# Low halves of the weights: subtracted on GpSimd, or written as -hi by ScalarE and completed by an adding DMA

## The chip, the cores and the metric

The kernel runs on one core of a Trainium2 chip. The metric is the device time of one execution in microseconds. A difference of 0.3% is about 8.7 us.

## The reference, cut to what matters

A trunk of four layers over 528 positions (16 learned tokens in front of 512 frames) of width 1024, in float32. Each layer is a mixer and an MLP, each with a norm ahead of it and a residual after it:

```python
for layer in range(4):           # mixers: DeltaNet, attention, RG-LRU, DeltaNet
    u = rmsnorm(h, norm_mix_w[layer])
    h = h + mixer[layer % 3](u)  # w_in, the mixer's own work, w_out
    u = rmsnorm(h, norm_mlp_w[layer])
    h = h + square(relu(u @ w1[layer])) @ w2[layer]   # 1024 -> 4096 -> 1024
return rmsnorm(h, final_norm_w)
```

Most of the work is the products with weight matrices.

## The kernel before

**Products in three passes.** A float32 product is made from rounded operands (type float32r): the weight W is split into hi, its rounded value, and lo = W - hi, and the activation x the same way. `part` (line 372) issues three matmuls for each block of 128 rows: hi with x's high part, hi with x's low part, lo with x's high part. The 528 positions are done in two halves of 264 columns, so a full unit of weights (128 partitions x 1024, eight blocks of 128 columns) is 8 x 3 x 2 = 48 matmuls.

**Where weights come from.** The host lays all weights out in rows of `wts`, each 128 partitions x 2 units x 1024. `load` (line 293) fetches one row, 1 MB, from SP's queue into one of two buffers `raw`. `wsplit` (line 300) makes hi and lo of one unit: ScalarE copies raw to hi (line 309), and one engine, VectorE or GpSimd, subtracts (line 310). For a full unit hi and lo are two buffers of the pool `wp`, which has seven buffers in rotation; the first product of an MLP (`w1`) runs a scheme of seven products on half-size blocks, and its hi and lo share one buffer.

**Who subtracts.** `prep` (line 313) takes VectorE for the first two rows, and for `w2`, `lru_in`, `lru_out` and `lru_gate` VectorE for the first unit of a row and GpSimd for the second (LO_ENG, line 47). All other full units (`dn_ba`, `dn_in`, `dn_out`, `da_in`, `da_out`) are GpSimd's. That makes 82 units for VectorE and 188 for GpSimd. The 188 are 64 of `w2`, 62 of `dn_in` and `dn_ba`, 24 of `da_in`, 16 of `dn_out`, 8 of `da_out`, 8 of `lru_in`, 4 of `lru_out` and 2 of `lru_gate`. The half-size blocks of w1 are split by VectorE, one of seven by GpSimd; these stay.

**How far ahead.** `unit` (line 352) calls `prep` until six buffers' worth are waiting. With seven buffers in rotation, the lo of a full unit among full units takes the buffer that the unit three before it gives up.

**The MLP.** `mlp` (line 591) runs four groups: eight w1 units, then eight `w2` units that contract the group's eight hidden tiles. `open` (line 363) begins the first two units of `w2` on the first six tiles before the last two hidden tiles are ready.

**Order.** The program is written with background generators (`tick`, line 230) that advance the mixers' own work while products run. A scheduler then fixes the order of each engine's instructions ahead of the run; on the chip each engine works through its list in order and waits on semaphores. DMAs are issued from SP's queue (weights, and a few small transfers of DeltaNet through DRAM), and from GpSimd's (the transfers `gd`, `sa` and `vs` of the mixers).

Of the kernel before, what the change touches and what calls it, by code (L numbers as in the profile page):

```python
# [9 lines left out]
F32 = mybir.dt.float32  # L10
F32R = mybir.dt.float32r
AF = mybir.ActivationFunctionType
ALU = mybir.AluOpType
# [30 lines left out]
LATS = [1.7] * 8 + [1.1]  # L44
CORE_DMA = "gggsss"

LO_ENG = {"w2": "vg", "lru_in": "vg", "lru_out": "vg", "lru_gate": "vg"}

PRODS = (11, 21, 2, 3, 4, 1, 22)
OUT_PARTS = {"dn_out": (4, 4), "da_out": (4, 4), "lru_out": (8,)}  # L50
# [97 lines left out]
class K:  # L148
# [148 lines left out]
        m = len(self.rows[r])  # L297
        self.nc.sync.dma_start(raw[:, :m], self.wts[r, :, :m, :])

    def wsplit(self, src, lo_eng, names):  # L300

        nc = self.nc
        n = src.shape[1]
        if n == 512:
            t = self.wp.tile([128, 1024], F32R, tag="w", name=names)
            hi, lo = t[:, :512], t[:, 512:]
        else:
            hi, lo = (self.wp.tile([128, 1024], F32R, tag="w", name=f"{k}{names}") for k in ("hi", "lo"))
        nc.scalar.copy(hi, src)  # L309
        lo_eng.tensor_tensor(lo, src, hi.bitcast(F32), ALU.subtract)  # L310
        return hi, lo

    def prep(self):

        if self.wnext >= len(self.items):
            return
        nc = self.nc
        r, k = self.items[self.wnext]
        self.wnext += 1
        self.load(r)  # L320
        raw = self.raws[r]
        unit = self.rows[r][0]
        if unit[0] != "w1":
            key = self.rows[r][k]
            eng = nc.vector if r < 2 or LO_ENG.get(key[0], "gg")[k] == "v" else nc.gpsimd
            self.wq.append((key, 2) + self.wsplit(raw[:, k], eng, f"{r}_{k}"))
        else:
            A11, A12, A21, A22 = raw[:, 0, :512], raw[:, 0, 512:], raw[:, 1, :512], raw[:, 1, 512:]
            if k == 0:
                self.s12 = [self.L1(self.getl()), self.L1(self.getl())]  # L330
            S1, S2 = self.s12
            add = lambda o, a, b, op: self.sadd(k).tensor_tensor(o, a, b, op)  # L332
            if k == 2:
                add(S1, A21, A22, ALU.add)
                add(S2, S1, A11, ALU.subtract)
            elif k == 3:
                add(A21, A11, A21, ALU.subtract)
            elif k == 6:
                add(A12, A12, S2, ALU.subtract)
            src = (A11, A12, S2, A21, A22, S1, A12)[k]  # L340
            eng = nc.vector if k != 3 else nc.gpsimd
            self.wq.append((unit + (k,), 1) + self.wsplit(src, eng, f"op{r}_{k}"))
        if k == 0:
            self.load(r + 1)
# [1015 lines left out]
```

## Time and profile before

| | |
|---|---|
| median of 3 runs | 2884.54 us (2882.99 to 2892.52) |
| the profiled execution | 2883.85 us, span 2882.1 us |
| TensorE (PE) busy | 94% of the span, mean granted clock 0.965 |
| VectorE (DVE), ScalarE (ACT), GpSimd (POOL) busy | 72%, 45%, 32% |
| DMA | 241.11 MB, mean 84 GB/s |

PE is TensorE's matmuls, PEld its weight loads. A name with q (SPq, POOLq) is that engine's sequencer, which issues DMAs and waits. The stages by time: first DeltaNet layer to about 430 us and its MLP to 830, attention to 1120 and its MLP to 1500, RG-LRU to 1740 and its MLP to 2080, second DeltaNet to 2500 and the last MLP to the end.

### The profile page before, as it was taken

To read this page: it belongs to the slowest core of one execution; us is meant where nothing else is said; L and a number is where in the kernel's file an instruction comes from. 1 tells how busy PE (TensorE), PEld (TensorE's weight loads), DVE (VectorE), ACT (ScalarE), POOL (GpSimd) and SP (SyncE) were. 2 spreads that over 40 slices of the span, in tenths; PEclk is the share of its full clock that TensorE was granted. 3 is DMA by queue.
4 is the path that set the end of the run, shared out by engine and by line. 5 is a ranking of instruction groups with operands and counts; after the bars stand their busy time and mean duration, and the time that the engine had idled before them with its cause. 6 is when DMAs were issued, how large, how long until landed. Compare 5 with 4: busy or idle time off the path is not lost. (4 is left out here: it accounts for less than half of the span.)

```text
span 2882.1 us, 54564 instructions
## 1 busy us (share of the span) xinstructions
PE 2717.7 (94%) x22032; PEld 2627.1 (91%) x22032; DVE 2064.5 (72%) x4424; ACT 1291.2 (45%) x2856; POOL 918.0 (32%) x580
## 2 busy tenths in 40 slices
PE   7899998999999998999999889999998989999998
PEld 7898898999988887999998889999988888899997
DVE  6987749667735557876668987776589685677764
ACT  4454436334534444543354654443444554444433
POOL 4534333121243333211134532211454343422213
PEclk9999899999999999999999999999999899999999
DMA  4322212233331120322332112232223221132322
GB/s 145 90 79 73 58 50 76 90 102 103 103 105 64 56 66 31 103 89 88 103 103 74 68 65 97 95 103 89 89 89 93 64 67 52 52 103 95 110 89 74
DMA packets 74508, 241.11 MB, mean 84 GB/s; under 512 B 42278, under 2 KB 42824, under 8 KB 49040
## 3 DMA queue, kind: packets, MB, share of 16 engines
q1 hardware_dynamic: 68112, 222.46, 23.3%
q0 software_dynamic: 5488, 13.98, 2.0%
q8 instruction: 173, 2.83, 0.4%
q10 hardware_dynamic: 656, 1.18, 0.1%
q14 instruction: 79, 0.65, 0.1%
HBM read 229.23 MB, written 11.01 MB: 83 GB/s over the span
## 5 line engine op out<-in xcount | busy, mean ns | idle before, releaser
L310 POOL TENSOR_TENSOR lo<-raw,hi 128x1024 fp32r<-128x1024 f32 x188 | 460.0, 2447 | 836.2 <-PE d L219 450.1
L219 PE MATMUL c<-s,hi 128*128 128x264 f32 (+1 forms) x2768 | 511.7, 284 | 0.0
L219 PE MATMUL d<-s,hi 128*128 128x264 f32 (+1 forms) x2480 | 475.7, 289 | 36.1 <-DVE s L646 22.7
L309 ACT CAST hi<-raw 128x1024 fp32r<-128x1024 f32 x270 | 282.9, 1050 | 412.4 <-PE d L219 217.6
L219 PE MATMUL d<-uh,hi 128*128 128x264 f32 (+1 forms) x1520 | 453.9, 299 | 11.0 <-DVE s L646 10.9
L219 PE MATMUL d<-ul,hi 128*128 128x264 f32 (+1 forms) x1520 | 449.4, 296 | 0.0
L219 PE MATMUL d<-uh,lo 128*128 128x264 f32 (+1 forms) x1520 | 448.2, 295 | 0.0
L219 PEld LDWEIGHTS d<-s,hi 128*128 128x128 f32 x2480 | 391.9, 191 | 44.1 <-DVE s L646 19.0
L219 PEld LDWEIGHTS c<-s,hi 128*128 128x128 f32 x2768 | 430.1, 189 | 0.0
L219 PE MATMUL c<-s,lo 128*128 128x264 f32 (+1 forms) x1384 | 392.1, 284 | 0.0
L219 PE MATMUL d<-s,lo 128*128 128x264 f32 (+1 forms) x1240 | 357.4, 288 | 0.0
L219 PEld LDWEIGHTS d<-uh,hi 128*128 128x128 f32 x1520 | 298.2, 196 | 21.7 <-DVE s L646 14.1
L310 POOL TENSOR_TENSOR op<-raw,op 128x512 fp32r<-128x512 f32 x64 | 114.8, 1793 | 593.0 <-ACT op L309 582.0
L219 PEld LDWEIGHTS d<-uh,lo 128*128 128x128 f32 x1520 | 297.5, 196 | 5.0 <-issue 4.2
L219 PEld LDWEIGHTS d<-ul,hi 128*128 128x128 f32 x1520 | 297.8, 196 | 4.5 <-issue 3.5
L309 ACT CAST op<-raw 128x512 fp32r<-128x512 f32 x320 | 193.2, 619 | 237.2 <-PE c L219 119.4
L219 PEld LDWEIGHTS c<-s,lo 128*128 128x128 f32 x1384 | 261.1, 189 | 0.0
L219 PE MATMUL d<-s,op 128*128 128x264 f32 (+1 forms) x1788 | 242.2, 285 | 8.2 <-ACT s L485 3.8
L219 PEld LDWEIGHTS d<-s,lo 128*128 128x128 f32 x1240 | 237.4, 191 | 1.7 <-issue 1.5
L219 PEld LDWEIGHTS d<-s,op 128*128 128x128 f32 x1788 | 227.7, 190 | 9.7 <-ACT s L485 4.2
L310 DVE TENSOR_TENSOR op<-raw,op 128x512 fp32r<-128x512 f32 x256 | 222.4, 869 | 18.8 <-ACT op L309 18.7
L597 DVE TENSOR_TENSOR h<-h,c 128x264 f32<-128x264 f32 (+1 forms) x169 | 71.8, 425 | 184.2 <-PE c L219 184.0
(269 smaller groups left out, 5734.7 us busy)
## 6 DMA issues: line engine op xcount, KB each, us to landing
raw<-in_wts_dram SPq DMA_DIRECT2D x197, 1024.0 KB
s<-dimg SPq DMA_DIRECT2D x32, 245.0 KB
s<-gd POOLq DMA_DIRECT2D x16, 265.0 KB, 4.5
sa<-s POOLq DMA_DIRECT2D x16, 245.0 KB, 3.2
vs<-vd POOLq DMA_DIRECT2D x1, 2620.0 KB, 19.9
h<-in_hT_dram SPq DMA_DIRECT2D x8, 264.0 KB
s<-vs POOLq DMA_DIRECT2D x8, 264.0 KB, 3.0
raw<-in_wts_dram SPq DMA_DIRECT2D x4, 512.0 KB
```

Source lines behind the costliest of these rows:

```text
L219: return self.nc.tensor.matmul(out, lhsT=lhsT, rhs=rhs, start=start, stop=stop)
L309: nc.scalar.copy(hi, src)
L310: lo_eng.tensor_tensor(lo, src, hi.bitcast(F32), ALU.subtract)
L597: nc.vector.tensor_tensor(h, h, ps, ALU.add)
```

## The change

For the 188 units, GpSimd's subtraction goes. ScalarE, having written hi, writes -hi into the lo buffer, and an adding DMA issued from GpSimd's queue reads the same unit of weights from HBM a second time and adds it there: lo = -hi + W. VectorE's 82 units stay as they are.

```diff
-LO_ENG = {"w2": "vg", "lru_in": "vg", "lru_out": "vg", "lru_gate": "vg"}
+LO_ENG = {"w2": "vd", "lru_in": "vd", "lru_out": "vd", "lru_gate": "vd"}
...
-    def wsplit(self, src, lo_eng, names):
+    def wsplit(self, src, lo_eng, names, dram=None):
...
         nc.scalar.copy(hi, src)
-        lo_eng.tensor_tensor(lo, src, hi.bitcast(F32), ALU.subtract)
+        if dram is None:
+            lo_eng.tensor_tensor(lo, src, hi.bitcast(F32), ALU.subtract)
+        else:
+            nc.scalar.activation(lo, hi.bitcast(F32), AF.Copy, scale=-1.0)
+            nc.gpsimd.dma_start(lo, dram, accum_op=ALU.add)
         return hi, lo
...
-            eng = nc.vector if r < 2 or LO_ENG.get(key[0], "gg")[k] == "v" else nc.gpsimd
-            self.wq.append((key, 2) + self.wsplit(raw[:, k], eng, f"{r}_{k}"))
+            dram = None if r < 2 or LO_ENG.get(key[0], "dd")[k] == "v" else self.wts[r, :, k, :]
+            self.wq.append((key, 2) + self.wsplit(raw[:, k], nc.vector, f"{r}_{k}", dram))
```

## Rows read from the trace of the kernel before

**Rows 1.** The page, busy time of each engine, share of the span, instructions.

```profile
PE 2717.7 (94%) x22032; PEld 2627.1 (91%) x22032; DVE 2064.5 (72%) x4424; ACT 1291.2 (45%) x2856; POOL 918.0 (32%) x580
```

**Rows 2.** Stretches: length; PE, PEld, DVE, ACT, POOL busy; clock; DMA share; GB/s.

```profile
35.00:400.00 365.00, 331.57 (x2880) 315.05 (x2880) 280.10 (x805) 171.86 (x555) 151.57 (x109) 0.92 0.25 69
600.00:700.00 100.00, 100.00 (x823) 100.00 (x822) 68.13 (x115) 39.05 (x63) 20.75 (x10) 1.00 0.29 96
1600.00:1700.00 100.00, 76.18 (x540) 73.92 (x539) 91.98 (x99) 56.33 (x82) 46.05 (x26) 0.86 0.18 64
```

**Rows 3.** Groups by form: shapes, count, busy us, mean ns, idle before, its releasers.

```profile
L310 POOL TENSOR_TENSOR lo<-raw,hi 128x1024 fp32r<-128x1024 f32 x188 | 460.0, 2447 | 836.2 <-PE d L219 450.1 <-PE c L219 213.4 <-issue 69.7
L309 ACT CAST hi<-raw 128x1024 fp32r<-128x1024 f32 x270 | 282.9, 1050 | 412.4 <-PE d L219 217.6 <-PE c L219 111.9 <-DMA raw<-in_wts_dram 58.6
L310 DVE TENSOR_TENSOR lo<-raw,hi 128x1024 fp32r<-128x1024 f32 x82 | 119.4, 1457 | 51.1 <-PE c L219 30.6 <-PE d L219 14.7 <-issue 2.3
```

**Rows 4.** Waits of SP's queue over the span: us in total, times, longest.

```profile
SPq L298 <- POOL lo L310: 1224.7, 125, 28.3
```

**Rows 5.** PE's waits, 35 to 400 us: first and last of 18 rows.

```profile
PE d L219 <- DVE s L646: 4.0, 4, 3.1
...
PE c L219 <- ACT l L890: 0.2, 1, 0.2
```

**Rows 6.** PE's waits, 1500 to 1760 us: the longest.

```profile
PE d L219 <- DVE s L646: 22.7, 6, 7.1
```

**Rows 7.** Timeline of one MLP group: start us, length us, instruction, idle before it.

```profile
586.73 1.06 ACT L309 CAST hi<-raw 128x1024 fp32r<-128x1024 f32 x1 [1.67 <-PE c L219]
...
588.38 3.49 POOL L310 TENSOR_TENSOR lo<-raw,hi 128x1024 fp32r<-128x1024 f32 x1 [5.81 <-ACT l L578]
...
596.41 0.31 PEld L219 LDWEIGHTS d<-s,hi 128*128 128x128 f32 x2
...
602.55 2.41 POOL L310 TENSOR_TENSOR lo<-raw,hi 128x1024 fp32r<-128x1024 f32 x1 [10.68 <-PE c L219]
602.57 1.05 ACT L309 CAST hi<-raw 128x1024 fp32r<-128x1024 f32 x1 [3.18 <-PE c L219]
...
603.72 0.31 PEld L219 LDWEIGHTS c<-s,hi 128*128 128x128 f32 x2
...
604.08 1.96 DVE L310 TENSOR_TENSOR lo<-raw,hi 128x1024 fp32r<-128x1024 f32 x1 [0.35 <-PE c L219]
...
609.55 0.31 PEld L219 LDWEIGHTS c<-s,hi 128*128 128x128 f32 x2
...
609.85 2.41 POOL L310 TENSOR_TENSOR lo<-raw,hi 128x1024 fp32r<-128x1024 f32 x1 [4.89 <-PE d L219]
...
615.75 1.23 DVE L310 TENSOR_TENSOR lo<-raw,hi 128x1024 fp32r<-128x1024 f32 x1 [2.54 <-PE c L219]
```

**Rows 8.** The page, DMA queues: packets, MB, share of 16 engines' span.

```profile
q1 hardware_dynamic: 68112, 222.46, 23.3%
q0 software_dynamic: 5488, 13.98, 2.0%
```

**Rows 9.** The page, DMA issues: count, KB each, median us to landing.

```profile
vs<-vd POOLq DMA_DIRECT2D x1, 2620.0 KB, 19.9
s<-vs POOLq DMA_DIRECT2D x8, 264.0 KB, 3.0
```

**Rows 10.** Groups by form: a DMA issue on POOL, and a two-input operation of VectorE.

```profile
L858 POOL DMA_DIRECT2D s<-sa x16 | 16.0, 998 | 18.5 <-DMA sa<-s 18.2 <-issue 0.2
L639 DVE SCALAR_TENSOR_TENSOR s<-s,cols,s 128x528 f32<-128x528 f32 x168 | 148.7, 892 | 9.2 <-ACT s L637 6.2 <-ACT s L635 1.9
```

**Rows 11.** One line's instructions: duration ns min/median/max, first and last start.

```profile
L639 DVE SCALAR_TENSOR_TENSOR s<-s,cols,s x168: 661/759/4665, 36.6 to 2360.4; 128x528 f32<-128x528 f32 x168
L310 DVE TENSOR_TENSOR lo<-raw,hi x82: 1158/1223/3065, 12.8 to 2842.7; 128x1024 fp32r<-128x1024 f32 x82
```

**Rows 12.** Groups by form on POOL, 35 to 400 us: GpSimd's subtraction.

```profile
L310 POOL TENSOR_TENSOR lo<-raw,hi 128x1024 fp32r<-128x1024 f32 x30 | 73.8, 2459 | 119.1 <-PE d L219 75.7 <-issue 27.0 <-PE c L219 15.0
```

## The prediction

> **What bounds the kernel now.** I read the busy shares first. TensorE is busy 94% of the span, VectorE 72%, ScalarE 45%, GpSimd 32% [rows 1], so what does not delay TensorE costs nothing. Then the table by stretches, because a share is a mean over stages. In an MLP TensorE is busy 100.00 of 100 us at clock 1.00, with GpSimd at 20.75; in the first DeltaNet layer it is busy 331.57 of 365 us with VectorE at 280.10; in the RG-LRU layer it falls to 76.18 of 100 and VectorE leads with 91.98 [rows 2]. Third, the groups: GpSimd's 188 subtractions take 460.0 us, 2.447 us each, and the idle time ahead of them (836.2 us) ends mostly in "PE d" and "PE c", that is, in a matmul that gives a buffer back [rows 3]. So GpSimd waits for TensorE there, not the other way round. Among the waits of TensorE in the first DeltaNet layer and in RG-LRU I found VectorE's results on top, and GpSimd's subtraction nowhere: 18 rows, from 4.0 us down, together 33 us in the first DeltaNet layer, nearly all of them for VectorE [rows 5], and 22.7 us for one wait in RG-LRU [rows 6]. The subtraction that goes is hidden. What can be gained or lost is in how soon the lo buffer is full after TensorE frees it, and in what the change does to VectorE and to the DMAs.
>
> **The window.** One group of `w2` in the timeline [rows 7] shows the time allowed. A full unit takes TensorE 609.55 - 603.72 = 5.83 us. The second unit's lo starts at 588.38 and its matmuls at 596.41: 8.0 us. The fourth unit's lo starts at 602.55, the moment the first unit's buffer comes free, and its matmuls at 609.55: 7.0 us (short, because the first two units were begun early and little of them was left). The sixth unit's lo starts at 609.85 and is wanted two units after 609.55, at 621.2: 11.4 us, and the eighth's window is alike. The third matmul of a unit is the first to use lo, so 0.2 us more is free. GpSimd's 2.41 us fits in each of these many times.
>
> **The change part by part.**
>
> *Taken away:* 188 x 2.447 = 460 us of GpSimd, cost on the path nothing [rows 3].
>
> *Added on ScalarE:* 188 writes of -hi. The nearest row is the copy of the same shape, 1.050 us [rows 3]; 188 x 1.05 = 197 us, ScalarE from 45% to 52%. What is queued behind one: the next hi, and the mixers' activations. The next hi is due at the same moment (the copy at 602.57 starts beside the subtraction at 602.55), so each may be 1.05 us late; it has a unit more of slack. I charge nothing for that. The step is on the new chain, though: 1.05 us before the DMA can be issued, or 2.1 us if the scheduler puts the next hi first.
>
> *Added on GpSimd:* 188 issues. The nearest row is 0.998 us [rows 10]: 188 us in place of 460. An issue waits for ScalarE where the subtraction waited for TensorE; behind it in the MLP is only the one subtraction per row of w1, in the mixers the transfers of DeltaNet.
>
> *Added on the DMA engines:* 188 x 512 KB = 98.6 MB of weights read again, and each transfer must read the buffer too before it writes the sum. No adding DMA stands in this trace, so I bound issue to landing by near rows. A plain 264 KB from GpSimd's queue lands in 3.0 us [rows 9]. SP's queue moved 222.46 MB in 23.3% of 2882 us, 331 GB/s while busy; GpSimd's queue 13.98 MB in 2.0%, 243 GB/s [rows 8]. A transfer of 264 KB at 331 GB/s is 0.8 us, which leaves 2.2 us fixed. Counted as 1 MB (read twice): at 331 GB/s 3.2 + 2.2 = 5.4 us; at 243 GB/s 4.3 + 2.2 = 6.5 us; at the slowest row, 2620 KB in 19.9 us or 132 GB/s [rows 9], 7.9 + 2.2 = 10.1 us. If reading the buffer costs nothing the low end is 1.6 + 2.2 = 3.8 us. I take 6.5 us, from the same queue.
>
> The Trainium skill (DMA: Bandwidth & Descriptors, Anatomy of one DMA) gives a fit for such a transfer, 2.0 us and the bytes at 436 GB/s. By it 512 KB would be an estimated 3.2 us, or 4.4 us if the bytes count twice, and every window would hold; no row here shows an adding transfer, so that is left to the rival in which all is hidden.
>
> *The chain against the windows.* -hi 1.05, semaphore about 0.1, DMA 6.5: 7.65 us. At the fourth unit (7.0 + 0.2) that is 0.45 us late. A row of weights is also in flight there: raw is freed by the last reader, SP's load waits 1224.7 us in all for GpSimd's subtraction [rows 4], and now will wait for ScalarE and VectorE. The row of units five and six is freed when VectorE's subtraction of 604.08 ends, about 606, inside the new transfer (about 605 to 609). Sharing the engines with 1 MB (3.2 us) makes it between 0 and 3.2 us later; I take 1.0. So 1.5 us x 16 groups = 24 us (bounds: 0; with 10.1 us and full sharing 7.3 us, 117 us). At the second unit 7.65 is inside 8.2 and only sharing hurts: 0.5 x 16 = 8 us (bounds 0 and 16 x 3.0 = 48). At the sixth and eighth, 11.4 covers it: nothing, and it would need a landing above 10.3 us to show.
>
> *Stretches in which both units of a row are completed by DMA.* In `dn_out` and `da_out`, 24 units, unit follows unit, and the engines are asked for 2 x 4.3 + 3.2 = 11.8 us per two units of 5.83 us: just full. I take 0.5 us per unit, 12 us (bounds: 0; at 7.9 us per transfer 19.0 - 11.7 = 7.3 per pair, 88 us). In DeltaNet's heads 30 units stand in 365 us [rows 12], 12.2 us each with the other work between them, so a window is twice as long; attention is mixed in the same way.
>
> *DeltaNet's own transfers* (`gd`, `sa`, `s`) go through the same queue, behind 512 KB in flight some of the time. Sixteen heads: a delay of one to four us each, partly covered: 1 us x 16 = 16 us (bounds 0 and 64).
>
> *Given back by VectorE.* Its subtraction took 1.96 us at 604.08, while GpSimd's ran, and 1.23 us at 615.75 alone [rows 7]. Over the span it has a mean of 1.457 us against a median of 1.223: 82 x 0.234 = 19 us; the convolution's step 0.892 against 0.759: 168 x 0.133 = 22 us [rows 3, 10, 11]. With smaller groups like these some 60 us of VectorE's time is stretch, part of it by the work of GpSimd that stays. Where TensorE waits for VectorE (taking the second DeltaNet layer like the first, 2 x 33, and 23 us in RG-LRU: 89 us at most) I let a bit under a quarter come back: 20 us (bounds 0 and 40).
>
> Sum: 24 + 8 + 12 + 16 - 20 = +40 us. Against the profiled execution's 2883.85 us (0.7 us under the median of the runs) that is 2924 us, 1.4% more.
>
> **The rivals.**
>
> *The transfer is hidden, and VectorE is freed: faster.* The price is VectorE's stretch alone, 30 us: 2854 us. For it speaks that no window is under 7.0 us and that TensorE's waits are on VectorE. It decides where landing is under about 5.5 us, so that 1.05 + 0.1 + 5.5 stays in 7.2, and DeltaNet's transfers keep their slack. Against it: only the low half of my bounds gives that. The Trainium skill (SBUF — State Buffer, Who interferes with whom) says that a VectorE instruction with two inputs from SBUF contends with a GpSimd instruction that reads SBUF; the two subtractions of 1.96 and 1.23 us agree.
>
> *Hidden and nothing given back: the same,* 2876 to 2892 us. The time goes nowhere because the stretch of VectorE is made by GpSimd's other work, or small delays cancel it.
>
> *The adding DMA is slow: much slower.* With a landing of 10 us or more the DMA engines, not TensorE, set the pace: 16 x (4.1 + 3.1) = 115 us in the groups of `w2`, 88 us in `dn_out` and `da_out`, the 64 us of DeltaNet's own transfers: about +267, 3151 us. It decides from a landing of about 9 us on. For it: each packet is read, added and written back, which no row prices. Against it: the queues' rates of 243 and 331 GB/s.
>
> **How the numbers follow.** 0.3% (8.7 us) is about what a measurement can tell here. Partly hidden with stalls at the edges, my forecast: 0.42, 2895 to 3000 us, 2924. Slow DMA: 0.20, 3000 to 3200. The same: 0.13. Faster: 0.25, 2835 to 2875. So slower 0.62, same 0.13, faster 0.25. The range leaves out the lower third of the faster case and the upper half of the slow one: 2855 to 3100; the forecast's own is 2895 to 3000.
>
> **What would show each step.** Right: TensorE waiting for "DMA lo" inside the groups of `w2`, first at the fourth unit, some 1 to 3 us each time; GpSimd's busy time down by about 270 us and ScalarE's up by 197; VectorE's subtraction near 1.23 us on the mean; landing of the adding DMA between 5.4 and 8 us; SP's loads no longer waiting for GpSimd. The forecast is wrong if the landing is under 5.5 us (then TensorE keeps 100 of 100 us in the MLP and the time falls), or over 9 us (then the stretches with both units by DMA lengthen most).

## The result and the profile after

The changed kernel takes 2859.09 us (median of 4 runs, 2851.11 to 2862.83) beside 2887.62 us for the kernel before on the same chip: a ratio of 0.9897, 95% interval 0.9866 to 0.9929. That is 1.0% faster. The forecast was 2924 us, slower; the time lies just inside the wide range (2855 to 3100) and outside the forecast's own (2895 to 3000), on the side to which it gave 1 chance in 4. The profiled run of after is 2855.45 us with a span of 2853.7 us. All comparisons here and below leave out one execution of a later kernel (the one with idle writes), which took 4978.56 us where its others took 2853.03 to 2866.44.

The page of after: busy time of the engines, the two DMA queues that carry the weights, and the issues that go through GpSimd's queue (count, KB each, median us to landing).

```profile
PE 2700.2 (95%) x22032; PEld 2612.2 (92%) x22032; DVE 1853.9 (65%) x4424; ACT 1459.4 (51%) x3046; POOL 622.0 (22%) x580
...
q1 hardware_dynamic: 68112, 222.46, 23.0%
q0 software_dynamic: 32560, 112.56, 22.2%
...
lo<-in_wts_dram POOLq DMA_DIRECT2D x188, 512.0 KB, 5.9
...
s<-gd POOLq DMA_DIRECT2D x16, 265.0 KB, 5.0
sa<-s POOLq DMA_DIRECT2D x16, 245.0 KB, 4.3
```

Against [rows 1] GpSimd is down by 296 us (forecast 272) and ScalarE up by 168 (forecast 197; the writes alone are 199.3). The surprise is VectorE, whose instructions are the same 4424: 1853.9 us in place of 2064.5, that is 210.6 us less. Groups by form of after (count, busy us, mean ns, idle before), to set beside [rows 3, 10]:

```profile
L313 ACT ACTIVATE lo<-hi 128x1024 fp32r<-128x1024 f32 x188 | 199.3, 1060 | 372.1 <-PE d L219 276.7 <-PE c L219 94.5
L314 POOL DMA_DIRECT2D lo<-in_wts_dram x188 | 165.7, 881 | 1004.8 <-ACT lo L313 698.2 <-DVE h L601 175.9 <-DVE l L581 36.0
L311 DVE TENSOR_TENSOR lo<-raw,hi 128x1024 fp32r<-128x1024 f32 x82 | 105.4, 1287 | 20.6 <-PE d L219 10.4 <-issue 4.7 <-ACT hi L309 2.8
L643 DVE SCALAR_TENSOR_TENSOR s<-s,cols,s 128x528 f32<-128x528 f32 x168 | 134.4, 811 | 11.7 <-ACT s L641 6.2 <-ACT s L639 4.4
L581 DVE SCALAR_TENSOR_TENSOR l<-l,rb 128x264 f32<-128x264 f32 x48 | 20.2, 425 | 0.0
L1129 DVE TENSOR_SCALAR l<-l,soa 128x128 f32<-128x128 f32 x32 | 7.0, 282 | 0.3
L801 DVE TENSOR_TENSOR eg<-s,ngc 106x5 f32<-106x5 f32 x16 | 4.9, 308 | 10.5 <-DMA s<-gd 10.5
```

The last three stood so in the kernel before, four lines higher in the code:

```profile
L577 DVE SCALAR_TENSOR_TENSOR l<-l,rb 128x264 f32<-128x264 f32 x48 | 40.7, 849 | 0.0
L1125 DVE TENSOR_SCALAR l<-l,soa 128x128 f32<-128x128 f32 x32 | 17.7, 615 | 0.3
L797 DVE TENSOR_TENSOR eg<-s,ngc 106x5 f32<-106x5 f32 x16 | 13.3, 829 | 3.8 <-DMA s<-gd 3.8
```

They take half of what they took, or less, with nothing about them changed. The best single sight of the cause is one instruction of the `w2` group of [rows 7], in the timeline of before: GpSimd's subtraction ran from 588.38 for 3.49 us, and this one, 0.43 us on the mean in after, took 2.30 beside it.

```profile
589.86 2.30 DVE L577 SCALAR_TENSOR_TENSOR l<-l,rb 128x264 f32<-128x264 f32 x1
```

**By stage.** I cut both spans where GpSimd does its step (`rt<-ms,nhalf`) of the norm ahead of each mixer and each MLP, so a mixer's stage takes in its out-projection; the first DeltaNet layer of before ends at 470 us by this cut, not at the "about 430" given ahead. The columns are those of [rows 2]: stretch, length, then busy time. The three recurrent stages of before (DeltaNet 1, RG-LRU, DeltaNet 2), with the first MLP second:

```profile
29.24:470.49 441.25, 400.95 (x3422) 382.42 (x3420) 332.29 (x907) 209.79 (x624) 183.73 (x127) 0.93 0.24 68
470.49:831.34 360.85, 359.25 (x2938) 357.79 (x2938) 250.03 (x431) 151.45 (x252) 84.42 (x47) 1.00 0.29 95
1522.21:1733.29 211.08, 179.61 (x1363) 175.86 (x1361) 194.83 (x219) 115.01 (x176) 96.49 (x60) 0.93 0.20 71
2088.13:2528.45 440.32, 398.63 (x3411) 378.67 (x3410) 331.59 (x906) 206.15 (x620) 182.49 (x128) 0.93 0.25 71
```

and the same of after:

```profile
28.84:458.57 429.73, 395.84 (x3422) 377.80 (x3420) 285.93 (x907) 242.68 (x661) 125.88 (x127) 0.94 0.51 115
458.57:826.01 367.44, 361.84 (x2938) 359.30 (x2938) 231.52 (x431) 167.57 (x271) 54.07 (x48) 1.00 0.43 123
1528.39:1728.17 199.78, 177.48 (x1363) 173.16 (x1361) 174.60 (x219) 129.50 (x191) 75.52 (x60) 0.95 0.41 103
2084.42:2500.23 415.81, 383.80 (x3415) 366.03 (x3413) 281.74 (x907) 242.62 (x661) 125.77 (x129) 0.96 0.53 120
```

DeltaNet 1 gives 11.5 us, RG-LRU 11.3, DeltaNet 2 24.5: 47.3 us. The four MLPs and attention take back 6.6 + 2.5 + 1.4 - 0.7 + 9.0 = 18.8 us. The difference, 28.5 us, is the 28.4 us between the two profiled runs, but for the ends of the spans. In the recurrent stages I also took the length less TensorE's busy time, its idle: 113.5 us before, 88.2 after, 25.3 us less. The rest of the gain there is busy time of the same matmuls, which were granted a clock of 0.94 to 0.96 where before had 0.93. What TensorE waits for changed too: its waits for VectorE's results in the three stages add up to 90.2 us before and 56.0 after. The largest of them in RG-LRU (us in total, times, longest), to set beside [rows 6]; `c` and `d` are the accumulators that a matmul writes:

```profile
PE d L219 <- DVE s L650: 11.5, 5, 4.2
```

TensorE's waits for the new transfer, over the whole span of after (us in total, times, longest), and SP's waits beside [rows 4]:

```profile
PE d L219 <- DMA lo<-in_wts_dram: 10.7, 2, 8.6
PE c L219 <- DMA lo<-in_wts_dram: 2.2, 6, 0.9
```

```profile
SPq L298 <- DVE op L311: 920.1, 64, 44.9
SPq L298 <- DVE lo L311: 664.0, 78, 20.7
SPq L298 <- ACT hi L309: 585.4, 47, 28.3
```

Only 12.9 us, two thirds of it one wait of 8.6 us where attention begins. GpSimd is gone from the list of what SP's loads (L298) wait for.

### The profile page after: what moved, and what is told of

It reads as the page before. It is cut to its first block, busy times and chain, and to the rows that moved or that the text cites. A ratio compares the mean times of both kernels' runs of the same rounds, so it can differ in the third digit from the quotient of the medians.

```text
span 2853.7 us, 54820 instructions
## 1 busy us (share of the span) xinstructions
PE 2700.2 (95%) x22032; PEld 2612.2 (92%) x22032; DVE 1853.9 (65%) x4424; ACT 1459.4 (51%) x3046; POOL 622.0 (22%) x580
## 3 DMA queue, kind: packets, MB, share of 16 engines
q0 software_dynamic: 32560, 112.56, 22.2%
## 5 line engine op out<-in xcount | busy, mean ns | idle before, releaser
L219 PE MATMUL d<-s,hi 128*128 128x264 f32 (+1 forms) x2480 | 476.4, 288 | 23.1 <-DVE s L650 11.5
L313 ACT ACTIVATE lo<-hi 128x1024 fp32r<-128x1024 f32 x188 | 199.3, 1060 | 372.1 <-PE d L219 276.7
L314 POOL DMA_DIRECT2D lo<-in_wts_dram x188 | 165.7, 881 | 1004.8 <-ACT lo L313 698.2
L219 PEld LDWEIGHTS d<-uh,hi 128*128 128x128 f32 x1520 | 300.0, 197 | 22.7 <-DVE s L650 12.9
L219 PEld LDWEIGHTS d<-uh,lo 128*128 128x128 f32 x1520 | 298.8, 197 | 15.9 <-DMA lo<-in_wts_dram 11.2
L311 DVE TENSOR_TENSOR op<-raw,op 128x512 fp32r<-128x512 f32 x256 | 196.0, 766 | 31.9 <-ACT op L309 31.4
```

Of the source, the lines that this page charges most:

```text
L219: return self.nc.tensor.matmul(out, lhsT=lhsT, rhs=rhs, start=start, stop=stop)
L313: nc.scalar.activation(lo, hi.bitcast(F32), AF.Copy, scale=-1.0)
L314: nc.gpsimd.dma_start(lo, dram, accum_op=ALU.add)
```

## Experiments

Theory A: GpSimd's subtraction, which reads two operands from SBUF, held up VectorE's instructions; in the recurrent mixers, where TensorE waits for VectorE, that cost time, and taking it away is the whole gain, while the adding DMA itself costs some. Rivals: the gain is a chance of the order that the scheduler chose; or it is GpSimd's queue and the raw buffers that come free. Ratios are to the kernel before in the same session.

**Half and half.** Two kernels split the 188 units by stage: one sends the units of DeltaNet and RG-LRU by DMA and leaves attention and `w2` to GpSimd's subtraction, the other does the opposite. (The units are 92 and 96; the expectations call them 94 each.)

```diff
...
+            if e == "d" and not (key[0][:3] in ("dn_", "lru")):
+                e = "g"
...
```

> The adding DMA only for DeltaNet's and RG-LRU's units (94 of 188); attention's and w2's 94 go back to GpSimd. Theory A (the gain is VectorE freed from GpSimd's reads where VectorE holds TensorE up, which is in the recurrent mixers; the 20 us lost in the MLPs and attention come from the transfer being late): the stages add, about 2840 us, 1.6% under the kernel before. Rival B (the gain is a chance of the new instruction order): no relation to the stages, anywhere from 2840 to 2890 us, with the DeltaNet layers not repeating 430 and 416 us.

> The complement: the adding DMA only for attention's and w2's units; DeltaNet and RG-LRU subtract on GpSimd. Theory A: the gain stays away and the losses stay, about 2905 us, 0.6% over the kernel before. Rival C (VectorE's relief in the MLPs pays too, through time that the mixers get): 2870 us or less. Rival B: no relation.

Measured: the recurrent half 2846.57 us, ratio 0.9861 (0.9839 to 0.9883), 12.5 us under the whole change, though the two intervals overlap; the other half 2900.46, ratio 1.0057 (1.0037 to 1.0076), slower than before. DeltaNet 1 and 2 and RG-LRU of the first:

```profile
29.49:453.82 424.33, 389.00 (x3422) 370.45 (x3420) 286.71 (x907) 242.42 (x661) 125.73 (x127) 0.96 0.51 117
1508.64:1708.74 200.10, 177.84 (x1363) 173.41 (x1361) 174.69 (x219) 129.48 (x191) 75.50 (x60) 0.95 0.40 103
2063.39:2483.98 420.59, 390.96 (x3415) 372.76 (x3413) 280.70 (x907) 243.50 (x661) 126.62 (x128) 0.94 0.52 119
```

TensorE's idle in them is 87.2 us, as in after (88.2); its MLPs sum to 1408.6 us beside 1411.2 before and 1421.0 after. In the second kernel the recurrent stages are those of before again: the second DeltaNet layer took

```profile
2098.20:2538.47 440.27, 397.67 (x3411) 377.80 (x3410) 332.58 (x906) 206.66 (x620) 183.33 (x128) 0.93 0.25 71
```

TensorE's idle in its three recurrent stages is 113.1 us, beside 113.5 before, and its waits there for VectorE's results are 90.5 us, beside 90.2; in the first kernel they are 59.5, beside 56.0 in after. So gain and loss have their places and follow the edit, stage by stage; a chance of the order is unlikely, since two kernels with different orders give the same idle in either case.

**Reads against writes.** To the changed kernel I added idle work on GpSimd after each of the 188 transfers; the output is unchanged, and one of the 34 working buffers `s` was given up for a scratch tile. One kernel subtracts hi from itself into the scratch, in two halves; the other writes zeros to the scratch five times, which keeps GpSimd longer but reads nothing.

```diff
...
+            for i in range(2):
+                h = hi.bitcast(F32)[:, i * 512:(i + 1) * 512]
+                nc.gpsimd.tensor_tensor(self.scr, h, h, ALU.subtract)
```

```diff
...
+            for i in range(5):
+                self.tc.keep_in_program_order(nc.gpsimd.memset(self.scr, 0.0))
```

> All of the change, and behind each adding DMA GpSimd also subtracts hi from itself into a scratch tile, two operations of 512 columns, about 2.6 us, read by nobody (one of the 34 working tiles is given up for the scratch). It brings GpSimd's reads of SBUF back and nothing else that the change took. Theory A: VectorE's busy time goes back from 1854 to about 2050 us and the time to 2880 to 2890 us. Rival D (the gain came because GpSimd's queue or the raw buffers come free sooner): the queue is as full as before, so it also goes to 2880; told apart from A by the next run. Rival B: stays near 2859 or goes anywhere.

> As the run with the idle subtraction, but GpSimd fills the scratch tile with zeros five times instead, about 2.5 us of GpSimd's time that reads nothing from SBUF. Theory A: VectorE stays near 1860 us busy and the time near 2860 us. Rival D (the queue's time): 2880 us, as with the subtraction.

Measured: reads 2902.09 us, ratio 1.0063 (1.0042 to 1.0084); writes 2863.01 (median of three), ratio 0.9913 (0.9886 to 0.994). The pages and groups of the two, reads first:

```profile
PE 2725.4 (94%) x22032; PEld 2632.2 (91%) x22032; DVE 1998.6 (69%) x4424; ACT 1459.3 (50%) x3046; POOL 1060.9 (37%) x956
...
L318 POOL TENSOR_TENSOR scr<-hi 128x512 f32<-128x512 f32 x376 | 449.7, 1196 | 247.8 <-ACT hi L310 236.1 <-issue 0.4
```

```profile
PE 2707.9 (95%) x22032; PEld 2618.8 (92%) x22032; DVE 1868.5 (65%) x4424; ACT 1456.8 (51%) x3044; POOL 1112.6 (39%) x1520
...
L317 POOL MEMSET scr<- 128x512 f32 x940 | 557.5, 593 | 38.5
```

GpSimd is busy 1061 us in one and 1113 us in the other, yet VectorE's same instructions take 1998.6 us beside the reads and 1868.5 beside the writes (1853.9 with neither). The second DeltaNet layer is back at 441.29 us with the reads, 422.64 with the writes. In the three recurrent stages TensorE's idle is 105.2 us with the reads and 89.5 with the writes, and its waits for VectorE's results are 76.3 and 60.8 us. So the reads bring back about two thirds of VectorE's stretch (144.7 of 210.6 us) and two thirds of the idle that had gone. I had expected VectorE near 2050 us and a time of 2880 to 2890 us. The time came out above that because the cost of the adding DMA stays: against before, MLPs and attention are 18.7 us longer and the recurrent stages only 2.7 us shorter. The rival of GpSimd's queue falls with the writes, which fill that queue too; the rival of the raw buffers falls with the reads, which do not touch them. Theory A is shown: it is the reads.

**What the DMA costs at the edges.** Two kernels looked for the part of attention and `w2` that could go by DMA without loss. One sends attention too, but for the input units of its first two heads, and leaves `w2` to GpSimd; the other sends only the sixth and eighth units of each `w2` group, whose windows are long.

```diff
...
+            if e == "d" and not (key[0] != "w2" and not (key[0] == "da_in" and key[2] % 8 < 2)):
+                e = "g"
...
```

```diff
...
+            if e == "d" and not (key[0][:3] in ("dn_", "lru") or key[0] == "w2" and key[2] >= 4):
+                e = "g"
...
```

> The adding DMA for DeltaNet, RG-LRU and attention, but attention's first six units (its first two heads) and all of w2 by GpSimd. Theory A says that attention's loss is one wait of 8.6 us at its start, where the 2620 KB transfer of the same queue shares the engines with the adding DMAs: the attention stage goes from 344.5 us back to 336 to 340, the MLPs stay at the times of before, and the whole is at 2840 to 2848 us. Rival: attention loses through its slower landings all along (median 7.1 us against 5.8 in the MLPs); then the stage stays at 344.

> The adding DMA for DeltaNet and RG-LRU, and in w2 only for the sixth and eighth unit of a group, which have 11.4 us; the second and fourth unit (8.0 and 7.0 us) and attention go back to GpSimd. Theory A: no matmul of an MLP waits for the adding DMA, and the four MLP stages add up to about 1409 us as in the run with DeltaNet and RG-LRU alone, not to the 1421 of the full change. Rival (the two adding DMAs and the reads slow the MLP in another way than by those two windows): about 1415 us.

Measured: 2857.3 us, ratio 0.9889 (0.9866 to 0.9911), and 2861.64 us in the one run of the other, too few for an interval. The first missed as a whole (2840 to 2848 was expected) and nearly held in its stage: attention took 340.41 us (344.46 in after, 339.40 with GpSimd), the wait of 8.6 us gone. The MLPs of the other sum to 1411.9 us, between the 1409 expected and the rival's 1415. That sum cannot decide, since a kernel without any DMA in its MLPs (VectorE in place of the DMA, below) has 1413.0; but no matmul waits for the transfer there, as theory A said. What spoiled the wholes is in the main the first DeltaNet layer, which runs the same matmuls in the three kernels: 424.33 us in the recurrent half, 434.20 and 441.32 in these two, with TensorE idle 35.3, 33.5 and 34.4 us. The row of the last:

```profile
29.20:470.52 441.32, 406.92 (x3422) 388.13 (x3420) 286.59 (x907) 243.38 (x661) 125.67 (x127) 0.91 0.50 112
```

The granted clock was 0.96, 0.93 and 0.91, a mean over stretches at TensorE's two levels of 2.4 and 1.2 GHz. So one stage moves by 17 us with its clock alone, and a stage's idle time is the steadier measure. Where the best place for the DMA in attention and `w2` lies can't be read from these totals.

**VectorE in place of the DMA.** If only GpSimd's reads hurt, VectorE can subtract by itself, with no second read of the weights: in DeltaNet and RG-LRU alone (the rest stays with GpSimd), or in all 188 units.

```diff
...
+            if e == "d":
+                e = "v" if key[0][:3] in ("dn_", "lru") else "g"
...
```

```diff
...
+            self.wq.append((key, 2) + self.wsplit(raw[:, k], nc.vector, f"{r}_{k}"))
...
```

> No adding DMA: DeltaNet's and RG-LRU's 94 units are subtracted by VectorE, the other 94 by GpSimd as before. In a DeltaNet layer VectorE gets about 38 x 1.22 = 46 us of work and loses the stretch of about the same size. If only the sum of VectorE's work counts there, the DeltaNet layers stay at 441 and 440 us and the time at 2885. If it counts that a short operation in a chain is held up by a whole subtraction of GpSimd, they come down part of the way, to about 430, and the time to 2860 to 2870.

> All 188 units subtracted by VectorE, no adding DMA and no GpSimd subtraction of a full unit. In the MLPs and attention nothing waited for GpSimd's reads, so little should change against the run with DeltaNet and RG-LRU by VectorE alone: 2820 to 2835 us; VectorE busy about 2036 + 94 x 1.22 - 90 of stretch = 2060 us. If VectorE becomes the bound in an MLP (250 us of 360 and 16 x 1.22 = 20 more), matmuls would wait for its subtraction and the MLPs grow by some us each.

Measured: 2828.27 us, ratio 0.9806 (0.9775 to 0.9837), and 2825.25, ratio 0.9784 (0.976 to 0.9807). My expectation of the first was too high by 30 us and more: the DeltaNet layers came to 414 and 413 us, not 430. The second lies in its range, VectorE is busy 2048.2 us (2060 was expected), and the MLPs do not grow (1409.6 us in all). The stages of the first:

```profile
29.59:443.80 414.21, 388.79 (x3422) 370.98 (x3420) 321.16 (x944) 210.35 (x624) 97.15 (x90) 0.96 0.26 73
1500.73:1708.93 208.20, 181.27 (x1362) 177.92 (x1361) 186.63 (x232) 118.63 (x178) 63.01 (x46) 0.91 0.21 72
2066.12:2478.87 412.75, 386.73 (x3415) 368.85 (x3413) 320.84 (x945) 208.54 (x623) 98.29 (x90) 0.95 0.26 75
```

In DeltaNet TensorE's idle falls to 25.4 and 26.0 us, where the DMA left 35.3 and 29.6, though VectorE has 34 to 40 us more to do. Of TensorE's waits, those for `s<-dimg` (DeltaNet's transfers back from DRAM, on SP's queue) differ most: 0.6 us here, 11.2 in the recurrent half and 11.7 in after. They were 8.1 us in before, where no adding DMA ran, so it is not shown that the DMA makes them. `gd` and `sa` land in 4.5 and 3.3 us against 5.4 and 4.3. In RG-LRU it is the other way: VectorE is nearly full (186.63 of 208.20 us) and the DMA's 200.10 us is better.

**Mixed.** So: DeltaNet by VectorE, RG-LRU (14 units) by DMA, attention and `w2` by GpSimd as before.

```diff
...
+            if e == "d":
+                e = {"dn_": "v", "lru": "d"}.get(key[0][:3], "g")
...
```

> DeltaNet's units by VectorE, RG-LRU's by the adding DMA, attention and w2 by GpSimd: each stage as in its best run so far. If the stages add: TensorE idle 25 us in a DeltaNet layer and 22 in RG-LRU (27 there with VectorE), RG-LRU's stage 200 us against 208, the whole about 2820 us. Rival: the difference in RG-LRU is the granted clock (0.95 against 0.91) and not the work; then 2828 us as with VectorE alone.

Measured: 2819.59 us, ratio 0.9769 (0.9743 to 0.9794), the shortest of all, 2.3% under before. RG-LRU took 199.13 us:

```profile
1504.89:1704.02 199.13, 178.94 (x1363) 174.32 (x1361) 174.81 (x219) 129.53 (x191) 74.79 (x60) 0.92 0.41 104
```

TensorE's idle in that stage is 20.2 us, against 26.9 with VectorE, at nearly the same clock (0.92 and 0.91). So the difference there is the work and not the clock, against the rival. The interval of the whole overlaps those of both kernels with VectorE, so which of the three is best is not settled by the totals.

**A read of one operand.** Again idle work on GpSimd in the changed kernel, the output unchanged: four copies of halves of hi, one operand each.

```diff
...
+            for i in range(4):
+                h = hi.bitcast(F32)[:, i % 2 * 512:i % 2 * 512 + 512]
+                nc.gpsimd.tensor_copy(self.scr, h)
```

> As the run with the idle subtraction, but GpSimd copies halves of hi into the scratch tile four times: reads of one operand in place of two. If any read of SBUF by GpSimd holds VectorE up: VectorE's busy time above 1950 us and the time near 2890 us. If it takes two operands: VectorE near 1868 and the time near 2862, as with the zeros.

Measured: 2986.1 us, ratio 1.0347 (1.0326 to 1.0369).

```profile
PE 2752.4 (92%) x22032; PEld 2658.7 (89%) x22032; DVE 2011.0 (67%) x4424; ACT 1462.7 (49%) x3046; POOL 1165.0 (39%) x1332
```

```profile
PE d L220 <- DMA lo<-in_wts_dram: 58.1, 18, 7.1
```

VectorE is stretched to 2011.0 us, so copies hold it up too. The time, far over the 2890 us expected for that, says less: the copies (594.4 us in all) also stood ahead of adding transfers in GpSimd's list, and TensorE waited 58.1 us for those. From issue to landing the median is 5.8 us still, so they were probably issued late. What a read of one operand costs in time stays open.

## Why the prediction was wrong

The forecast's sum was +40 us; the two profiled runs differ by -28.4 (the stages by -28.5). By place: the recurrent stages were to gain 20 and lose 16 for DeltaNet's transfers and 8 for `dn_out` (16 of the 24 dense units), +4 in all, and they gave -47.3. The MLPs were to lose 32 and lost 9.8 (6.6 + 2.5 + 1.4 - 0.7). Attention was to lose 4 and lost 9.0.

**The step that failed is "Given back by VectorE".** It took the stretch as some 60 us, from a few groups, and let 20 us of it come back. The stretch that went was 210.6 us: I had priced long instructions, at nearly 1.2 times their median; the short ones, unpriced, had taken two to three times what they take in after (the three groups shown above), and some 130 of the 210 us lie in groups with a mean under 0.7 us. `eg<-s,ngc` is the plainest: it went from 829 ns to 308 on the mean, and ScalarE waited 25.7 us for it in before and 1.7 in after. The waits of TensorE for VectorE were taken rightly (89 us; 90.2 measured, though the 22.7 us of [rows 6] are six waits and not one), but 34.2 us of them came back where the term has 20. With the other waits, which grew, TensorE idles 25.3 us less in the recurrent stages. Its busy time fell as well, by 22.1 us (979.2 to 957.1), at the higher granted clock; of that the forecast had nothing. Mechanism right, size less than half of the real one: 20 us against 47.3, from which what the transfers cost there is already taken off.

The Trainium skill (SBUF — State Buffer, Who interferes with whom) says that a VectorE instruction with two inputs in SBUF contends with a GpSimd instruction that reads SBUF and not with one that only writes. The reads and the writes agree, 1998.6 us against 1868.5. It says too that an instruction with at most one such input does not contend outside the 2-port perf modes, and counts `tensor_scalar` among those that can enter such a mode. `l<-l,soa` is a `tensor_scalar`, 615 ns before and 282 after, so it was held up; which mode it ran in no run shows.

**The second error is the edges of `w2`**, 24 + 8 = 32 us. The MLPs lengthened by 9.8 us, and the matmuls of `w2` waited only 2.2 us for the transfer, in six waits of 0.9 us at the longest. (One more wait of 2.1 us, at 814.7 us, stands inside the first MLP's stretch, but is the start of attention's input product.) The transfer landed in 5.9 us, not 6.5, and sharing with the loads of rows, for which I had added 1 us a group, seldom showed (in the first MLP the median is 5.8 us, the longest 8.2). The 0.1 us for the semaphore was short: the issue starts 0.3 us after ScalarE's write ends, on the median of 135 that waited for it. One of them in after:

```profile
598.21 1.06 ACT L313 ACTIVATE lo<-hi 128x1024 fp32r<-128x1024 f32 x1 [3.82 <-PE d L219]
...
599.57 0.86 POOL L314 DMA_DIRECT2D lo<-in_wts_dram  x1 [5.92 <-ACT lo L313]
```

1.06 + 0.3 + 5.9 = 7.3 us is about the 7.2 of the shortest window, and the stalls are tenths of a us.

**The dense out-projections**, 12 us: no such wait stands among TensorE's. Attention does lose 9.0 us, 8.4 of them idle time, but for a reason I had not listed. The timeline of after where attention starts:

```profile
822.31 1.13 POOL L1017 DMA_DIRECT2D vs<-vd  x1 [1.67 <-issue]
...
827.52 0.94 POOL L314 DMA_DIRECT2D lo<-in_wts_dram  x1 [0.31 <-ACT lo L313]
...
829.90 0.86 POOL L314 DMA_DIRECT2D lo<-in_wts_dram  x1 [1.45 <-ACT lo L313]
```

`vs`, 2620 KB, is under way in the same queue for some 20 us (what waits for it starts at 842.56) when two adding transfers are issued. Adding transfers of this stretch (826 to 860 us) land in 12.4 us on the median and 17.0 at most, and TensorE waits 8.6 us, once. With GpSimd subtracting the first six units the wait was gone.

**DeltaNet's own transfers**, 16 us: in part borne out. They land later (`gd` 0.5 us, `sa` 1.1), and with VectorE in the DMA's place the two layers' idle is 13.5 us less than in the recurrent half (65.0 to 51.4). How much of that is these transfers no run tells.

**Right:** the landing (5.9 us; 5.4 to 8 was given, and the bound that counts the buffer as read again, 5.4, is nearest); ScalarE's writes (199.3 us for 197); GpSimd's issues (165.7 us for 188, 881 ns each); VectorE's subtraction (1.287 us, toward 1.23); SP no longer waiting for GpSimd. What happened is in the main the rival "hidden, and VectorE is freed", whose 2854 us was near, partly by luck: it had 30 us given back and nothing lost, where 47.3 came back and 18.8 went. I gave it 0.25 because it wanted a landing under 5.5 us; its own window leaves 7.2 - 1.15 = 6.05, and 5.9 was short enough.

The Trainium skill (DMA: Bandwidth & Descriptors, Anatomy of one DMA) would have given an estimated 3.2 or 4.4 us for the landing; the measured 5.9 decides.

**Open:** why TensorE's granted clock is higher in the recurrent stages when it idles less there. The two go together in most of these runs, but the same matmuls with the same idle ran at 0.96 and at 0.91, so idle time alone does not set it, and no run tells cause from chance. Two waits of after show one way in which idle can cost more than its length. Up to the wait of 2.1 us that ends at 814.74 the clock was 1.00 (from 805.0 to 812.3 us), behind it 0.51, the lower level (814.8 to 818.1), then 1.00 again (818.4 to 822.0). Behind the wait of 8.6 us it was 0.50 (844.6 to 848.8), then 1.00 (849.2 to 852.0).

## What to carry to other kernels

Before pricing the work that goes off an idle engine, price what it did to its neighbour: take minimum, median and maximum of the short instructions of the neighbour's whole list, not of its few longest groups, and look where another engine waits for them. Here the cheapest cure was not the elaborate one: the subtraction on VectorE, with no more instructions and no second read, beat the adding DMA (2825 against 2859 us), and in these runs the DMA did better than VectorE only in the one stage where VectorE is nearly full (199 to 200 us against 208). Compare stages by the idle time of the engine that sets the pace, since the clock alone moved one stage by 17 us.

## What the runs showed of the hardware

An adding transfer of 512 KB from HBM into SBUF takes 0.88 us of GpSimd to issue and lands in 5.3 us at least, 5.9 on the median and 17.0 at most. GpSimd's queue went from 2.0% to 22.2% of 16 engines' span for 98.6 MB more: about 576 us, 171 GB/s if the bytes count once, 342 if the buffer's read counts too, which is near the 331 GB/s of the plain loads [rows 8].

A VectorE instruction can be held for as long as a GpSimd instruction beside it runs. Of the 16 `eg<-s,ngc` of before nine took 0.15 us. The other seven, 0.91 to 3.53 us, began during, or just before, a subtraction of GpSimd, and all seven ended with it to within 0.05 us. The timelines of before at two of them, GpSimd's rows and VectorE's:

```profile
2142.05 1.22 POOL L790 TENSOR_TENSOR s<-s,cst 106x530 f32<-106x530 f32 x1
2143.22 2.36 POOL L310 TENSOR_TENSOR lo<-raw,hi 128x1024 fp32r<-128x1024 f32 x1
...
2142.08 3.53 DVE L797 TENSOR_TENSOR eg<-s,ngc 106x5 f32<-106x5 f32 x1
...
221.38 2.71 POOL L310 TENSOR_TENSOR lo<-raw,hi 128x1024 fp32r<-128x1024 f32 x1 [3.42 <-PE d L219]
...
222.21 1.92 DVE L797 TENSOR_TENSOR eg<-s,ngc 106x5 f32<-106x5 f32 x1 [0.35 <-DMA s<-gd]
```

2142.08 + 3.53 is 2145.61, and 2143.22 + 2.36 is 2145.58: two GpSimd instructions in a row were sat out. 222.21 + 1.92 is 224.13, and 221.38 + 2.71 is 224.09. An operation of 106x5 elements took longer than VectorE's own subtraction of 128x1024 does alone (1.23 us [rows 7]).
